# Attention in a hybrid decoder trunk: query norm factor moved into the exponential, head norm scales folded into keys and cosines, squares in one pass, two splits issued earlier

## The chip, the cores and the metric

The kernel runs on one core of one Trainium2 chip. The metric is the device time of one execution in microseconds (us). The engines are named as in the profile: PE (TensorE matmul; PEld its weight loads), DVE (VectorE), ACT (ScalarE), POOL (GpSimd) and SP (SyncE, which issues most DMAs).

## What is computed

Two layers over a sequence of 256 tokens of width 1024, in float32. Each layer has a SwiGLU feed-forward block, a token mixer and a second SwiGLU block. The mixer of layer 0 is a diagonal state-space model, that of layer 1 is attention with 8 heads of 128 columns. The change touches the attention alone:

```python
qkv = (h @ w_qkv).reshape(bsz, seq, 3, N_HEADS, HEAD_DIM)
q = rms_norm(qkv[:, :, 0], q_gain)      # over the 128 columns of each head
k = rms_norm(qkv[:, :, 1], k_gain)
q = partial_rope(q, cos, sin) * (HEAD_DIM ** -0.5)   # rotates columns 0..31
k = partial_rope(k, cos, sin)
...
s_own = jnp.einsum('bqhd,bkhd->bqhk', q_c, k_own)
s_own = jnp.where(causal, s_own, -jnp.inf)
...
p = jax.nn.softmax(jnp.concatenate(scores, axis=-1), axis=-1)
```

With 256 tokens there is one block of keys, so what is left of the block-sparse form is plain causal attention.

## The kernel before

Six stages follow one another: feed-forward, state-space mixer, feed-forward, feed-forward, attention, feed-forward. All large products keep float32 accuracy by splitting: a weight tile becomes a rounded high half `whi` and the rest `wlo`, the activations likewise `xa`, and a product is three matmuls (high by high, low by high, high by low).

Weights come by `Stream` (lines 37 to 117). A unit is a raw tile of 128x2048 that a DMA fills; it has two halves of 1024 columns. `split` (line 74) makes a half's `whi` on ACT (line 92, or line 86 where no norm scale is multiplied in) and its `wlo` on DVE (line 93 or 87). For the attention's first six weights each of these is two instructions of 128x512. In this text a split is such a pair on DVE with its pair on ACT. `pump` (line 103) does the next split ahead of its use if a buffer is free; nine pairs of buffers exist. Engines work through their own instruction lists in order, and the lists are written in the order in which the Python code runs: there is no scheduler behind it.

The attention stage is `moba` (line 1256). Its first part is twelve chunks, numbered 0 to 11 here: first half of the heads' keys, first half of the queries, second half of the keys, second half of the queries, two halves of the values, each for two blocks of 128 tokens (`QKV`, line 214). A chunk is eight steps `k` of three 512-column matmuls (`product`, line 429, matmuls at lines 439 to 441) and takes PE some 5.6 us without other work. After steps 1 and 5 `pump` splits one more half. Odd steps have hooks: four slots per chunk at which other work is put in, by the table `plan` (lines 1364 to 1378).

After a key or query chunk ACT evicts the product as `qs` (line 1278) and squares it head by head with a running sum (line 1282); POOL turns the four sums into norm factors `qrs` by six small instructions (line 1283 and `rsq`, lines 310 to 314). One chunk later, at the third slot, `rope` runs on DVE: four instructions scale each head by its factor and the norm scale (line 1293), six rotate the first 32 columns (lines 1299 to 1304). One further chunk later, at the third slot, `qk_tr` transposes the result on PE (line 1314; the last one a slot earlier) and ACT evicts it.

From chunk 6 on heads are added, each by `scores` (PE, then mask and maxima on DVE, lines 1324 to 1328), `expo` one slot later (two exponentials on ACT with sums), `normal` three slots after `scores` (reciprocal and two multiplications on DVE, lines 1343 to 1345), `p_tr` six slots after it (transposes of the probabilities on PE, line 1351, evicted by ACT) and `p_v` (product with the values). The second part of the stage, `mo`, is the output product.

```python
            for i in range(8):
                at(4 * (i + 1) + 2, rope, *prods[i])
                at(4 * (i + 2) + (2 if i < 7 else 1), qk_tr, *prods[i])
            for hd in range(8):
                g = 24 + 4 * hd if hd < 4 else 30 + 2 * hd
                for i, fn in ((0, scores), (1, expo), (3, normal), (6, p_tr)):
                    at(g + i, fn, hd)
```

Of the kernel before, what the change touches and what calls it, by code (L numbers as in the profile page):

```python
# [10 lines left out]
F32 = mybir.dt.float32  # L11
F32R = mybir.dt.float32r
AF = mybir.ActivationFunctionType
OP = mybir.AluOpType
AX = mybir.AxisListType
# [6 lines left out]
EPS = 1e-6  # L22
RAW = 3
HB = 9
NEG = -3.0e38
TWO_PI = 2.0 * math.pi
MAGIC = 12582912.0

# [92 lines left out]
def trunk_kernel(ctx: ExitStack, tc, x, ffn_norm, ffn_w_gate, ffn_w_up, ffn_w_down, mix_norm,  # L121
# [3 lines left out]
    nc = tc.nc  # L125
# [118 lines left out]
    cosT = cst[:, 256:288].rearrange("p (t f) -> p t f", t=2)  # L244
    sinT = cst[:, 288:320].rearrange("p (t f) -> p t f", t=2)
# [183 lines left out]
    def product(o, t, uA, uB, hooks, pumps=(1, 5)):  # L429

        for k in range(8):
            for f in hooks.get(k, ()):
                f()
            u = (uA, uB)[k // 4]
            wh, wl = st.get(u, (k % 4) // 2)
            c = slice((k % 2) * 512, (k % 2) * 512 + 512)
            ts = slice(t * 128, t * 128 + 128)
            xh, xl = X["h"][:, k, ts], X["l"][:, k, ts]
            mm(o, xh, woven(wh[:, c]), start=k == 0, stop=False)
            mm(o, xl, woven(wh[:, c]), start=False, stop=False)  # L440
# [815 lines left out]
    def moba(nxt):  # L1256
        V, P = nc.vector, nc.gpsimd
        SCL = 128 ** -0.5
        with tc.tile_pool(name="moba", bufs=1) as wp:
            gq = wp.tile([128, 2, 128], F32, name="gq")  # L1260
            for i, g in enumerate((moba_q_norm, moba_k_norm)):
                nc.sync.dma_start(gq[:, i, :], bass.AP(tensor=g.tensor, offset=g.offset,
                                                       ap=[[0, 128], [1, 128]]))
            vs = [wp.tile([128, D], F32, name=f"vs{t}") for t in range(2)]
            oa = wp.tile([128, 4224], F32R, name="oa")
            oh, ol = (oa[:, OO + 2048 * i:OO + 2048 * i + 2048].rearrange("p (k c) -> p k c", c=256)
                      for i in range(2))
            qkT, QS, QN, SC, PR, PT = {}, {}, {}, {}, {}, {}

            def chunk(kind, hh, t, hooks):  # L1270
                uA, uB = where[kind, hh, 0], where[kind, hh, 1]
                ps = psM()
                product(ps, t, uA, uB, hooks)
                if kind == "v":
                    nc.scalar.activation(halves(vs[t][:, hh * 512:(hh + 1) * 512]), unwoven(ps), AF.Identity, scale=Rr[t])
                    return
                qs = fp.tile([128, 512], F32, name="qs", tag="gr", bufs=2)
                nc.scalar.activation(halves(qs), unwoven(ps), AF.Identity, scale=Rr[t])
                ss = wp.tile([128, 4], F32, name="qss", bufs=2)
                sq = wp.tile([128, 128], F32, name="qsq", bufs=1)  # L1280
                for i in range(4):
                    nc.scalar.activation(sq, qs[:, i * 128:(i + 1) * 128], AF.Square, accum_out=ss[:, i:i + 1])
                P.tensor_scalar(ss, ss, 1.0 / 128, EPS, op0=OP.mult, op1=OP.add)
                rs = wp.tile([128, 4], F32, name="qrs", bufs=2)
                rsq(rs, ss, 4)
                QS[kind, hh, t] = (qs, rs)

            def rope(kind, hh, t):
                qs, rs = QS.pop((kind, hh, t))
                qn = wp.tile([128, 4, 128], F32, name="qn", bufs=2)  # L1290
                g = gq[:, 0 if kind == "q" else 1, :]
                for i in range(4):
                    V.scalar_tensor_tensor(qn[:, i, :], qs[:, i * 128:(i + 1) * 128], rs[:, i:i + 1], g,
                                           op0=OP.mult, op1=OP.mult)
                x1, x2 = qn[:, :, 0:16], qn[:, :, 16:32]
                cb = cosT[:, t, None, :].to_broadcast([128, 4, 16])
                sb = sinT[:, t, None, :].to_broadcast([128, 4, 16])
                m = [wp.tile([128, 4, 16], F32, name=f"rp{i}", bufs=1) for i in range(4)]
                V.tensor_tensor(m[0], x1, cb, op=OP.mult)
                V.tensor_tensor(m[1], x2, sb, op=OP.mult)  # L1300
                V.tensor_tensor(m[2], x2, cb, op=OP.mult)
                V.tensor_tensor(m[3], x1, sb, op=OP.mult)
                V.tensor_tensor(x1, m[0], m[1], op=OP.subtract)
                V.tensor_tensor(x2, m[2], m[3], op=OP.add)
                QN[kind, hh, t] = qn
# [11 lines left out]
            def scores(hd):  # L1317
                hh, i = divmod(hd, 4)
                q, k = qkT["q", hh], qkT["k", hh]
                ps = psA(i)  # L1320
                mm(ps[:, 0:128], q[:, i, 0:128], k[:, i, 0:128], start=True, stop=True)
                mm(ps[:, 128:384], q[:, i, 128:256], k[:, i, 0:256], start=True, stop=True)
                dv = ps.rearrange("p (a c) -> p a c", c=256)[:, :, 0:128]
                V.tensor_tensor(dv, dv, cmask[:, None, :].to_broadcast([128, 2, 128]), op=OP.add)
                mx = wp.tile([128, 2], F32, name="mx", bufs=3)
                V.reduce_max(mx[:, 0:1], ps[:, 0:128], axis=AX.X)
                V.reduce_max(mx[:, 1:2], ps[:, 128:384], axis=AX.X)
                V.tensor_scalar(mx, mx, -SCL, None, op0=OP.mult)
                SC[hd] = (ps, mx)

            def expo(hd):
                ps, mx = SC.pop(hd)
                pr = wp.tile([128, 384], F32, name="pr", bufs=4)
                sm = wp.tile([128, 2], F32, name="sm", bufs=4)
                nc.scalar.activation(pr[:, 0:128], ps[:, 0:128], AF.Exp, bias=mx[:, 0:1], scale=SCL,
                                     accum_out=sm[:, 0:1])
                nc.scalar.activation(pr[:, 128:384], ps[:, 128:384], AF.Exp, bias=mx[:, 1:2], scale=SCL,
                                     accum_out=sm[:, 1:2])
                PR[hd] = (pr, sm)

            def normal(hd):
                pr, sm = PR[hd]
                V.reciprocal(sm, sm)
                V.tensor_scalar(pr[:, 0:128], pr[:, 0:128], sm[:, 0:1], None, op0=OP.mult)
                V.tensor_scalar(pr[:, 128:384], pr[:, 128:384], sm[:, 1:2], None, op0=OP.mult)

            def p_tr(hd):
                pr, _ = PR.pop(hd)
# [30 lines left out]
            for i, (kind, hh, t) in enumerate(prods):  # L1379
                hooks = {2 * s + 1: plan.get((i, s), []) for s in range(4)}  # L1380
                if i == 0:
                    hooks.update(entry_hooks("moba"))
                chunk(kind, hh, t, hooks)
            acc = [None] * 4

            def mo(b, t, n, last=False):
# [165 lines left out]
```

## Time and profile before

| | |
|---|---|
| median of 3 runs | 921.55 us (921.38 to 924.65) |
| the profiled execution | 926.08 us |
| its span, first to last instruction | 924.3 us |
| mean granted TensorE clock | 0.997 |
| PE, PEld busy | 914.9 (99%), 817.9 (88%) |
| DVE, ACT, POOL busy | 719.0 (78%), 587.0 (64%), 222.7 (24%) |
| attention stage in the span | about 642 to 749 us |

Busy time is what the profiler saw an engine work; for PE the ends of matmuls are modelled and overlap, so that small gaps don't show there. A wait is idle time of an engine ahead of an instruction, put down to what released it. Times within the trace count from the span's start.

### The profile page before, as it was taken

To read this page: it belongs to the slowest core of one execution; us is meant where nothing else is said; L and a number is where in the kernel's file an instruction comes from. 1 tells how busy PE (TensorE), PEld (TensorE's weight loads), DVE (VectorE), ACT (ScalarE), POOL (GpSimd) and SP (SyncE) were. 2 spreads that over 40 slices of the span, in tenths; PEclk is the share of its full clock that TensorE was granted. 3 is DMA by queue.
4 is the path that set the end of the run, shared out by engine and by line. 5 is a ranking of instruction groups with operands and counts; after the bars stand their busy time and mean duration, and the time that the engine had idled before them with its cause. 6 is when DMAs were issued, how large, how long until landed. Compare 5 with 4: busy or idle time off the path is not lost.

```text
span 924.3 us, 15612 instructions
## 1 busy us (share of the span) xinstructions
PE 914.9 (99%) x5772; PEld 817.9 (88%) x5772; DVE 719.0 (78%) x1235; ACT 587.0 (64%) x1122; POOL 222.7 (24%) x389
## 2 busy tenths in 40 slices
PE   9999999999999999999999999999999999999998
PEld 7888878898999999999999999999888899999997
DVE  6899877868877888777678887776789668887773
ACT  7665756654376666666466666665898666676651
POOL 6992879924812000000020000001441020000000
PEclk9999999999999999999999999999999999999999
DMA  9999999988746766565637666563554647656531
GB/s 286 277 294 334 331 265 273 301 282 322 287 158 197 235 224 231 186 227 183 183 126 238 228 194 216 186 224 97 182 164 156 195 135 252 234 187 227 182 137 46
DMA packets 145388, 200.75 MB, mean 217 GB/s; under 512 B 20168, under 2 KB 117408, under 8 KB 145056
## 3 DMA queue, kind: packets, MB, share of 16 engines
q1 hardware_dynamic: 137744, 188.24, 62.6%
q0 software_dynamic: 6848, 10.72, 4.3%
q10 hardware_dynamic: 720, 0.80, 0.3%
q8 instruction: 45, 0.74, 0.3%
q14 instruction: 31, 0.25, 0.1%
HBM read 183.82 MB, written 15.76 MB: 216 GB/s over the span
## 4 chain that ended last, share of the span: by engine, by line
PE 89%; DMA 3%; POOL 2%; issue 2%; DVE 2%; ACT 1%; SPq 0%; ACTq 0%; DVEq 0%; POOLq 0%
PE pR L589 11%; PE pM L589 11%; PE pA L425 10%; PE pA L426 10%; PE pA L427 10%; PE pR L591 5%; PE pM L591 5%; PE pM L425 4%; PE pM L426 4%; PE pM L427 4%; PE pM L595 2%; PE pM L596 2%; PE pM L594 2%; DMA dA<-t 2%; PE pR L1118 1%
## 5 line engine op out<-in xcount | busy, mean ns | idle before, releaser
L93 DVE SCALAR_TENSOR_TENSOR wlo<-raw,gT,whi 128x512 fp32r<-128x512 f32 x328 | 228.0, 747 | 41.9 <-ACT whi L92 41.7
L87 DVE TENSOR_TENSOR wlo<-raw,whi 128x1024 fp32r<-128x1024 f32 (+1 forms) x155 | 188.0, 1233 | 41.4 <-ACT whi L86 37.0
L92 ACT ACTIVATE whi<-raw,gT 128x512 fp32r<-128x512 f32 x328 | 212.9, 710 | 3.5 <-PE pA L427 2.1
L86 ACT ACTIVATE whi<-raw 128x1024 fp32r<-128x1024 f32 (+1 forms) x155 | 158.5, 1045 | 38.3 <-DMA raw<-in_ffn_w_up_dram 25.5
L589 PE MATMUL pR<-xa,whi 128*128 128x512 f32 x456 | 174.2, 382 | 0.0
L589 PE MATMUL pM<-xa,whi 128*128 128x512 f32 x456 | 174.0, 382 | 0.0
L425 PE MATMUL pA<-whi,ah 128*128 128x512 f32 x352 | 134.9, 383 | 0.0
L426 PE MATMUL pA<-wlo,ah 128*128 128x512 f32 x352 | 133.7, 380 | 0.0
L427 PE MATMUL pA<-whi,al 128*128 128x512 f32 x352 | 133.6, 379 | 0.0
L591 PE MATMUL pR<-xa,wlo 128*128 128x256 f32 x456 | 124.3, 273 | 0.0
L591 PE MATMUL pM<-xa,wlo 128*128 128x256 f32 x456 | 124.3, 273 | 0.0
L355 POOL TENSOR_TENSOR ms<-ss 128x1 f32<-128x1 f32 x10 | 3.5, 348 | 435.4 <-ACT sq L352 435.4
L589 PEld LDWEIGHTS pR<-xa,whi 128*128 128x128 f32 x456 | 86.2, 189 | 12.2
L589 PEld LDWEIGHTS pM<-xa,whi 128*128 128x128 f32 x456 | 86.2, 189 | 11.9
L591 PEld LDWEIGHTS pM<-xa,wlo 128*128 128x128 f32 x456 | 87.4, 192 | 1.4
L591 PEld LDWEIGHTS pR<-xa,wlo 128*128 128x128 f32 x456 | 87.6, 192 | 0.0
L618 ACT ACTIVATE sg<-gr 128x256 f32<-128x256 f32 x66 | 27.5, 417 | 87.2 <-DVE gr L611 61.6
L425 PE MATMUL pM<-whi,xa 128*128 128x512 f32 (+1 forms) x208 | 79.9, 384 | 0.0
L426 PE MATMUL pM<-wlo,xa 128*128 128x512 f32 (+1 forms) x208 | 76.2, 366 | 0.1
L427 PE MATMUL pM<-whi,xa 128*128 128x512 f32 (+1 forms) x208 | 76.1, 366 | 0.0
L427 PEld LDWEIGHTS pA<-whi,al 128*128 128x128 f32 x352 | 66.7, 189 | 9.5
L425 PEld LDWEIGHTS pA<-whi,ah 128*128 128x128 f32 x352 | 66.8, 190 | 9.3
(290 smaller groups left out, 1745.1 us busy)
## 6 DMA issues: line engine op xcount, KB each, us to landing
raw<-in_ffn_w_down_dram SPq DMA_DIRECT2D x44, 1024.0 KB, 5.5
raw<-in_ffn_w_gate_dram SPq DMA_DIRECT2D x80, 512.0 KB, 4.0
raw<-in_ffn_w_up_dram SPq DMA_DIRECT2D x80, 512.0 KB, 5.1
raw<-in_moba_w_qkv_dram SPq DMA_DIRECT2D x12, 1024.0 KB, 5.2
TB<-dB SPq DMA_DIRECT2D x8, 768.0 KB, 7.0
dA<-blank SPq DMA_DIRECT2D x8, 512.0 KB, 10.2
dB<-tt POOLq DMA_DIRECT2D x16, 256.0 KB, 7.5
raw<-in_s_w_in_dram SPq DMA_DIRECT2D x4, 1024.0 KB, 9.7
```

The source lines that it names most:

```text
L86: nc.scalar.activation(hi[:, c], r[:, c], AF.Copy)
L87: nc.vector.tensor_tensor(lo[:, c], r[:, c], hi[:, c].bitcast(F32), op=OP.subtract)
L92: nc.scalar.activation(hi[:, c], r[:, c], AF.Identity, scale=g)
L93: nc.vector.scalar_tensor_tensor(lo[:, c], r[:, c], g, hi[:, c].bitcast(F32), op0=OP.mult, op1=OP.subtract)
L425: mm(o, xh, wh, start=start, stop=False)
L426: mm(o, xh, wl, start=False, stop=False)
L427: mm(o, xl, wh, start=False, stop=stop)
L589: mm(ps[i], a, XB[:, :, k, :].rearrange("p i (t c) -> p i c t", t=2), start=k == 0, stop=False, skip_group_check=True)
L591: mm(ps[i][:, 0:256], b, xh, start=False, stop=k == 7, skip_group_check=True)
L594: mm(o, a, xh, start=k == 0 and i == 0, stop=False, skip_group_check=True)
L595: mm(o, a, xl, start=False, stop=False, skip_group_check=True)
L618: nc.scalar.activation(sg, gr[:, 0, :], AF.Silu)
```

## The change

- The query's norm factor is no longer multiplied into the queries. It is a factor per token and head, so it goes into the scale of the exponential and into the maximum that is subtracted: POOL multiplies the factor by 128^-0.5 into `scl`, one instruction of 128x4 per query chunk.
- Both head norms' scales are folded: for columns 32 to 127 their product `gk` is multiplied into the keys alone; for the rotated columns each goes into its own copy of cosines and sines, `cs`. POOL makes both at the start of the stage, in ten instructions. So `rope` of a query chunk is the six rotations alone, and works in place on `qs`; `rope` of a key chunk still has the four scalings, with the product `gk`.
- The four squares with running sums become one ACTIVATE over 512 columns, and the sums a reduction on DVE.
- `normal` multiplies on ACT in place of DVE for heads 2 to 7; the reciprocal stays on DVE.
- Chunks 1 and 2 split one more half each, after step 3.
- The mask's value is -1e30 in place of -3e38, since it is now multiplied by a factor that differs from token to token.

```diff
+            gk = wp.tile([128, 128], F32, name="gk")
+            P.memset(gk[:, 0:32], 1.0)
+            P.tensor_tensor(gk[:, 32:128], gq[:, 0, 32:128], gq[:, 1, 32:128], op=OP.mult)
+            cs = wp.tile([128, 2, 4, 2, 16], F32, name="cs")
+            for i in range(2):
+                for m, (tr, c) in enumerate(((cosT, 0), (sinT, 16), (cosT, 16), (sinT, 0))):
+                    P.tensor_tensor(cs[:, i, m], tr, gq[:, i, None, c:c + 16].to_broadcast([128, 2, 16]), op=OP.mult)
...
-                sq = wp.tile([128, 128], F32, name="qsq", bufs=1)
-                for i in range(4):
-                    nc.scalar.activation(sq, qs[:, i * 128:(i + 1) * 128], AF.Square, accum_out=ss[:, i:i + 1])
+                sq = wp.tile([128, 512], F32, name="qsq", bufs=1)
+                nc.scalar.activation(sq, qs, AF.Square)
+                V.reduce_sum(ss, sq.rearrange("p (i c) -> p i c", c=128), axis=AX.X)
                 P.tensor_scalar(ss, ss, 1.0 / 128, EPS, op0=OP.mult, op1=OP.add)
                 rs = wp.tile([128, 4], F32, name="qrs", bufs=2)
                 rsq(rs, ss, 4)
+                if kind == "q":
+                    if t == 0:
+                        SQ[hh] = wp.tile([128, 4, 2], F32, name="scl", bufs=2)
+                    P.tensor_scalar(SQ[hh][:, :, t], rs, SCL, None, op0=OP.mult)
...
-                qn = wp.tile([128, 4, 128], F32, name="qn", bufs=2)
-                g = gq[:, 0 if kind == "q" else 1, :]
-                for i in range(4):
-                    V.scalar_tensor_tensor(qn[:, i, :], qs[:, i * 128:(i + 1) * 128], rs[:, i:i + 1], g,
-                                           op0=OP.mult, op1=OP.mult)
+                qn = qs.rearrange("p (i c) -> p i c", c=128)
+                if kind == "k":
+                    for i in range(4):
+                        V.scalar_tensor_tensor(qn[:, i, :], qn[:, i, :], rs[:, i:i + 1], gk, op0=OP.mult, op1=OP.mult)
...
-                V.tensor_scalar(mx, mx, -SCL, None, op0=OP.mult)
+                V.scalar_tensor_tensor(mx, mx, -1.0, SQ[hh][:, i, :], op0=OP.mult, op1=OP.mult)
...
-                nc.scalar.activation(pr[:, 0:128], ps[:, 0:128], AF.Exp, bias=mx[:, 0:1], scale=SCL,
+                nc.scalar.activation(pr[:, 0:128], ps[:, 0:128], AF.Exp, bias=mx[:, 0:1], scale=sc[:, 0:1],
                                      accum_out=sm[:, 0:1])
...
                 V.reciprocal(sm, sm)
-                V.tensor_scalar(pr[:, 0:128], pr[:, 0:128], sm[:, 0:1], None, op0=OP.mult)
-                V.tensor_scalar(pr[:, 128:384], pr[:, 128:384], sm[:, 1:2], None, op0=OP.mult)
+                for k, c in enumerate((slice(0, 128), slice(128, 384))):
+                    if hd < 2:
+                        V.tensor_scalar(pr[:, c], pr[:, c], sm[:, k:k + 1], None, op0=OP.mult)
+                    else:
+                        nc.scalar.activation(pr[:, c], pr[:, c], AF.Identity, scale=sm[:, k:k + 1])
...
-                chunk(kind, hh, t, hooks)
+                chunk(kind, hh, t, hooks, (1, 3, 5) if i in (1, 2) else (1, 5))
```

How this moves instructions on the engines is shown at three places.

The first is DVE in chunks 1 and 2, from the last split of chunk 0 on: `wlo` is a split, the `L1293` or `L1304` rows scale a key chunk, the rows after them (of six, the first is shown) rotate it. Before:

```order
L93 SCALAR_TENSOR_TENSOR wlo<-raw,gT,whi 128x512 x4
L1293 SCALAR_TENSOR_TENSOR qn<-qs,qrs,gq 128x128 x4
L1299 TENSOR_TENSOR rp_7453<-qn,cst 128x64
...
L93 SCALAR_TENSOR_TENSOR wlo<-raw,gT,whi 128x512 x4
L1293 SCALAR_TENSOR_TENSOR qn<-qs,qrs,gq 128x128 x4
```

With the change:

```order
L93 SCALAR_TENSOR_TENSOR wlo<-raw,gT,whi 128x512 x2
L1289 TENSOR_REDUCE qss<-qsq 128x4
L93 SCALAR_TENSOR_TENSOR wlo<-raw,gT,whi 128x512 x4
L1304 SCALAR_TENSOR_TENSOR qs<-qs,qrs,gk 128x128 x4
L1308 TENSOR_TENSOR rp_7468<-qs,cs 128x64
...
L93 SCALAR_TENSOR_TENSOR wlo<-raw,gT,whi 128x512 x2
L1289 TENSOR_REDUCE qss<-qsq 128x4
L93 SCALAR_TENSOR_TENSOR wlo<-raw,gT,whi 128x512 x4
L1304 SCALAR_TENSOR_TENSOR qs<-qs,qrs,gk 128x128 x4
```

Each chunk has a reduction between its splits, and two splits instead of one stand between that place and the scaling.

The second is DVE in chunk 6, where the second half of the keys is scaled while head 0's scores are masked and their maxima taken (`pA` is the scores' bank). Before:

```order
L93 SCALAR_TENSOR_TENSOR wlo<-raw,gT,whi 128x512 x2
L1324 TENSOR_TENSOR pA_7804<-pA_7804,cst 128x2x128
L1326 TENSOR_REDUCE mx<-pA_7804 128x1
L1327 TENSOR_REDUCE mx<-pA_7804 128x1
L1328 TENSOR_SCALAR mx<-mx 128x2
L93 SCALAR_TENSOR_TENSOR wlo<-raw,gT,whi 128x512 x2
L1293 SCALAR_TENSOR_TENSOR qn<-qs,qrs,gq 128x128 x4
```

With the change:

```order
L93 SCALAR_TENSOR_TENSOR wlo<-raw,gT,whi 128x512 x2
L1289 TENSOR_REDUCE qss<-qsq 128x4
L1333 TENSOR_TENSOR pA_7808<-pA_7808,cst 128x2x128
L1335 TENSOR_REDUCE mx<-pA_7808 128x1
L1336 TENSOR_REDUCE mx<-pA_7808 128x1
L1337 SCALAR_TENSOR_TENSOR mx<-mx,scl 128x2
L93 SCALAR_TENSOR_TENSOR wlo<-raw,gT,whi 128x512 x2
L1304 SCALAR_TENSOR_TENSOR qs<-qs,qrs,gk 128x128 x4
```

The reduction from which POOL makes the factors of the scaling stands directly ahead of the mask, behind a split.

The third is ACT in chunk 9, from the first exponential of head 3 to that of head 4. Before:

```order
L1335 ACTIVATE pr,sm<-pA_8076,mx 128x128
L1337 ACTIVATE pr,sm<-pA_8076,mx 128x256
L1353 ACTIVATE pT<-pR 128x384
L92 ACTIVATE whi<-raw,gT 128x512 x2
L1335 ACTIVATE pr,sm<-pA_8120,mx 128x128
```

With the change:

```order
L1345 ACTIVATE pr,sm<-pA_8068,mx,scl 128x128
L1347 ACTIVATE pr,sm<-pA_8068,mx,scl 128x256
L1366 ACTIVATE pT<-pR 128x384
L86 ACTIVATE whi<-raw 128x1024
L1358 ACTIVATE pr<-pr,sm 128x128
L1358 ACTIVATE pr<-pr,sm 128x256
L1345 ACTIVATE pr,sm<-pA_8112,mx,scl 128x128
```

Head 3's two normalizations stand ahead of head 4's exponential, and the split is already one of the next weight.

## Rows read from the trace of the kernel before

**Rows 1.** The page, busy time of each engine, share of the span, instructions
```profile
PE 914.9 (99%) x5772; PEld 817.9 (88%) x5772; DVE 719.0 (78%) x1235; ACT 587.0 (64%) x1122; POOL 222.7 (24%) x389
```

**Rows 2.** Waits of PE, 642 to 736 us: total, times, longest
```profile
PE pM L441 <- DVE wlo L93: 0.8, 3, 0.3
```

**Rows 3.** Timeline of PE: start, length, instruction, idle time ahead and releaser
```profile
655.70 0.38 PE L439 MATMUL pM<-whi,xa 128*128 128x512 f32 x1
655.91 0.38 PE L440 MATMUL pM<-whi,xa 128*128 128x512 f32 x1
656.54 0.48 PE L441 MATMUL pM<-wlo,xa 128*128 128x512 f32 x1 [0.24 <-DVE wlo L93]
...
695.38 0.38 PE L440 MATMUL pM<-whi,xa 128*128 128x512 f32 x1
696.08 0.48 PE L441 MATMUL pM<-wlo,xa 128*128 128x512 f32 x1 [0.33 <-DVE wlo L93]
```

**Rows 4.** Busy time by stretch: length, PE, PEld, DVE, ACT, POOL, clock, DMA, GB/s
```profile
642.20:700.00 57.80, 56.97 (x285) 48.57 (x284) 46.79 (x136) 52.73 (x139) 26.22 (x60) 1.00 0.50 159
700.00:735.00 35.00, 35.00 (x184) 30.80 (x183) 27.68 (x63) 24.23 (x54) 0.00 (x0) 1.00 0.48 163
```

**Rows 5.** Waits of DVE, 640 to 736 us
```profile
DVE qn L1293 <- POOL qrs L314: 5.7, 7, 0.9
```

**Rows 6.** Timeline of DVE, 651 to 688 us
```profile
651.26 1.42 DVE L93 SCALAR_TENSOR_TENSOR wlo<-raw,gT,whi 128x512 fp32r<-128x512 f32 x2 [2.81 <-ACT whi L92]
653.62 1.14 DVE L1293 SCALAR_TENSOR_TENSOR qn<-qs,qrs,gq 128x128 f32<-128x128 f32 x4 [0.94 <-POOL qrs L314]
...
655.74 2.73 DVE L93 SCALAR_TENSOR_TENSOR wlo<-raw,gT,whi 128x512 fp32r<-128x512 f32 x4
659.40 1.14 DVE L1293 SCALAR_TENSOR_TENSOR qn<-qs,qrs,gq 128x128 f32<-128x128 f32 x4 [0.93 <-POOL qrs L314]
...
678.87 1.41 DVE L93 SCALAR_TENSOR_TENSOR wlo<-raw,gT,whi 128x512 fp32r<-128x512 f32 x2
680.19 0.43 DVE L1324 TENSOR_TENSOR pA<-pA,cst 128x256 f32<-128x256 f32 x1
...
681.39 1.41 DVE L93 SCALAR_TENSOR_TENSOR wlo<-raw,gT,whi 128x512 fp32r<-128x512 f32 x2
683.16 1.14 DVE L1293 SCALAR_TENSOR_TENSOR qn<-qs,qrs,gq 128x128 f32<-128x128 f32 x4 [0.37 <-POOL qrs L314]
...
686.61 0.16 DVE L1343 RECIPROCAL sm<-sm 128x2 f32<-128x2 f32 x1
...
687.27 0.42 DVE L1324 TENSOR_TENSOR pA<-pA,cst 128x256 f32<-128x256 f32 x1
```

**Rows 7.** Timeline of ACT: first eviction, and last read of sums in chunks 0 and 5
```profile
648.19 0.69 ACT L1278 ACTIVATE qs<-pM,rr 128x512 f32<-128x512 f32 x1 [0.79 <-PE pM L441]
...
650.42 0.19 ACT L1282 ACTIVATION_READ_ACCUMULATOR qsq<-qs 128x1 f32 x1
...
678.92 0.19 ACT L1282 ACTIVATION_READ_ACCUMULATOR qsq<-qs 128x1 f32 x1
```

**Rows 8.** Groups of DVE by line: shape, count, busy, mean ns, idle before
```profile
L1327 DVE TENSOR_REDUCE mx<-pA 128x1 f32<-128x256 f32 x8 | 3.3, 414 | 0.0
```

**Rows 9.** Timeline of POOL: norm factors of chunk 0, power of chunk 1
```profile
650.70 0.20 POOL L1283 TENSOR_SCALAR qss<-qss 128x4 f32<-128x4 f32 x1 [3.57 <-ACT qsq L1282]
650.98 1.02 POOL L310 TENSOR_TENSOR qrs<-qss,nhalf 128x4 f32<-128x4 f32 x1
...
656.62 1.40 POOL L310 TENSOR_TENSOR qrs<-qss,nhalf 128x4 f32<-128x4 f32 x1
```

**Rows 10.** Group of ACT by line: shape, count, busy, mean ns, idle before
```profile
L1361 ACT ACTIVATE oa<-pR 128x256 fp32r<-128x256 f32 x8 | 3.1, 383 | 4.2 <-PE pR L1360 4.2
```

**Rows 11.** Timeline of PE: transposes of the second key chunk and of head 0
```profile
662.48 0.60 PE L1314 MATMUL pR<-cst,qn 128*128 128x128 f32 x4
...
687.50 0.49 PE L1351 MATMUL pR<-cst,pr 128*128 128x128 f32 x3
```

More of the change, by code (lines that the diff above doesn't have):

```diff
@@ L24 @@
 HB = 9
-NEG = -3.0e38
+NEG = -1.0e30
 TWO_PI = 2.0 * math.pi
@@ L1267, in moba, with chunk @@
                       for i in range(2))
-            qkT, QS, QN, SC, PR, PT = {}, {}, {}, {}, {}, {}
-            def chunk(kind, hh, t, hooks):
+            qkT, QS, QN, SC, PR, PT, SQ = {}, {}, {}, {}, {}, {}, {}
+            def chunk(kind, hh, t, hooks, pumps=(1, 5)):
                 uA, uB = where[kind, hh, 0], where[kind, hh, 1]
                 ps = psM()
-                product(ps, t, uA, uB, hooks)
+                product(ps, t, uA, uB, hooks, pumps)
                 if kind == "v":
@@ L1289, in rope @@
                 qs, rs = QS.pop((kind, hh, t))
-                qn = wp.tile([128, 4, 128], F32, name="qn", bufs=2)
-                g = gq[:, 0 if kind == "q" else 1, :]
-                for i in range(4):
-                    V.scalar_tensor_tensor(qn[:, i, :], qs[:, i * 128:(i + 1) * 128], rs[:, i:i + 1], g,
-                                           op0=OP.mult, op1=OP.mult)
+                qn = qs.rearrange("p (i c) -> p i c", c=128)
+                if kind == "k":
+                    for i in range(4):
+                        V.scalar_tensor_tensor(qn[:, i, :], qn[:, i, :], rs[:, i:i + 1], gk, op0=OP.mult, op1=OP.mult)
                 x1, x2 = qn[:, :, 0:16], qn[:, :, 16:32]
-                cb = cosT[:, t, None, :].to_broadcast([128, 4, 16])
-                sb = sinT[:, t, None, :].to_broadcast([128, 4, 16])
+                c1, s2, c2, s1 = (cs[:, "qk".index(kind), k, t, None, :].to_broadcast([128, 4, 16]) for k in range(4))
                 m = [wp.tile([128, 4, 16], F32, name=f"rp{i}", bufs=1) for i in range(4)]
[L1299 to L1302, printed above, removed]
+                V.tensor_tensor(m[0], x1, c1, op=OP.mult)
+                V.tensor_tensor(m[1], x2, s2, op=OP.mult)
+                V.tensor_tensor(m[2], x2, c2, op=OP.mult)
+                V.tensor_tensor(m[3], x1, s1, op=OP.mult)
                 V.tensor_tensor(x1, m[0], m[1], op=OP.subtract)
@@ L1332, in expo @@
                 ps, mx = SC.pop(hd)
+                sc = SQ[hd // 4][:, hd % 4, :]
                 pr = wp.tile([128, 384], F32, name="pr", bufs=4)
                 sm = wp.tile([128, 2], F32, name="sm", bufs=4)
-                nc.scalar.activation(pr[:, 0:128], ps[:, 0:128], AF.Exp, bias=mx[:, 0:1], scale=SCL,
+                nc.scalar.activation(pr[:, 0:128], ps[:, 0:128], AF.Exp, bias=mx[:, 0:1], scale=sc[:, 0:1],
                                      accum_out=sm[:, 0:1])
-                nc.scalar.activation(pr[:, 128:384], ps[:, 128:384], AF.Exp, bias=mx[:, 1:2], scale=SCL,
+                nc.scalar.activation(pr[:, 128:384], ps[:, 128:384], AF.Exp, bias=mx[:, 1:2], scale=sc[:, 1:2],
                                      accum_out=sm[:, 1:2])
```

## The prediction

> **What bounds the kernel now.** I read the page first: TensorE (PE) is busy in 99% of the span [rows 1]. Its busy time is modelled, so it hides small gaps, and the next view is who waits for whom on PE in the attention stage, 642 to 736 us. It lists one wait alone, 0.8 us in three places, on VectorE's (DVE) low half of a weight split [rows 2]. The third view, PE in order of time, shows what that view rounds away: two 512-column matmuls start 0.21 to 0.22 us apart, and in four places the product by the low half starts late. At 656.54 the step is 0.63 instead of 0.215, a loss of 0.41; at 668.10 and 682.19, read in the same way, 0.22 and 0.35; at 696.08 it is 0.70, a loss of 0.49 [rows 3]. Together 1.48 us, 0.16% of the time. All that the change touches lies in this stage, the clock stands at its upper level, 2.4 GHz, there (granted share 1.00, [rows 4]), and PE's own instructions keep their number and order. So the most that can be won is 1.48 us, and whatever is won or lost must show as a wait of PE.
>
> Why is DVE late in those places? It is busy 46.8 of 57.8 us, ScalarE (ACT) 52.7 [rows 4], and DVE's own longest wait is for GpSimd (POOL): 5.7 us in seven places, ahead of the head norm's scaling [rows 5]. The chain is: ACT evicts a product and squares it, POOL makes the norm factor, DVE scales and rotates, PE transposes one chunk later. The rows give DVE's prices, from start to start: a split 1.33 (678.87 to 680.19, rounded up), a scaling with its rotation 2.12 (653.62 to 655.74), of which the four scalings are 1.14 and the rotation 0.98, mask and maxima of one head 1.20 (680.19 to 681.39), reciprocal and two normalizations 0.66 (686.61 to 687.27) [rows 6].
>
> **The change, part by part.**
>
> Squares: four squares with running sums become one ACTIVATE over 512 columns. In the first chunk the four took from the eviction's end at 648.88 (648.19 + 0.69) to 650.61 (650.42 + 0.19), 1.73 us. The one costs at most the 0.69 of the eviction of the same size [rows 7], at least a quarter of the four, 0.43; I take 0.68 with its gap, so it ends at 649.56, 1.05 earlier. By itself none of that is on the path.
>
> The sum moves to DVE: eight new reductions of 128x512 into four numbers. The trace has none of this size; the nearest takes 0.41 for 256 elements [rows 8]. Ends: 0.41, as if length cost nothing, and 0.83, twice the row; it can't gain anything by itself. I take 0.62, halfway. What matters more is the place. The sum was ready as soon as ACT was; now POOL must wait until DVE comes to the reduction, behind the splits in its queue.
>
> Query chunks: four scalings go, 1.14 us of DVE each time, four times, and with them the rotation's wait for POOL. Key chunks keep both. The query's factor goes into the exponential's scale; the two extra operand reads and the four small POOL instructions have a whole stage of cover, so nothing.
>
> POOL's ten preparing instructions (the product of the two norm scales, the scaled cosines) stand ahead of the first norm factor. POOL was idle for 3.57 us before its first instruction of this kind, at 650.70 [rows 9], and ten of 0.2, as that one took, are 2.0. Held by splits for 0.4 each, as the power instruction was (1.40 - 1.02), they would be 6. I count nothing; the other end, 2.4 us, would delay the first key chunk and is kept for the range.
>
> Two more splits, one in chunk 1, one in chunk 2: 2.66 us of DVE work comes earlier, and from there each split is one chunk ahead of its use. This removes all four waits of [rows 3]: -1.48. But the rotation of the same chunk now stands behind two splits of its chunk instead of one, and its deadline has not moved.
>
> Normalization of heads 2 to 7 on ACT: DVE is relieved of some 0.5 per head (0.66 less the reciprocal's 0.16), ACT takes at most 2 x 0.38 by the copy of 256 columns [rows 10], covered by its idle time, 35.0 - 24.2 = 10.8 us after 700 [rows 4].
>
> **What is late next.** Two deadlines of PE: the transposes of the second key chunk at 662.48, and those of head 0's probabilities at 687.50 [rows 11]; without the earlier losses of 0.41 and of 0.99 they stand at 662.07 and 686.51. DVE's list from the first reduction to the end of head 0's normalization is now 14 splits (18.62), 4 scalings with rotation (8.48), 2 rotations (1.96), 6 reductions (3.72), one head's maxima (1.20) and normalization (0.66): 34.64 us. To it come waits for POOL at the four key chunks. From the squares' end to the scaling POOL's chain took 653.62 - 650.61 = 3.0 with one split beside it and 683.16 - 679.11 = 4.05 with two splits and a head's maxima [rows 6, 7]; I take 3.4, between them and nearer the first, since the third of the four new chains again has one split beside it. DVE fills 2.66, 2.66, 1.33 and 2.53 of the four chains with splits and maxima, so it waits 0.74 + 0.74 + 2.07 + 0.87 = 4.42.
>
> To test the method, the list before: from 651.26, 12 splits, 6 scalings with rotation, maxima and normalization are 30.54, the waits 0.94 at 653.62, 0.93 in the four chunks from 659.40 on and 0.37 at 683.16, in sum 5.03; that ends at 686.83, and the row says 687.27 [rows 6]. It is 0.44 short, which I add.
>
> The list after: 649.56 + 34.64 + 4.42 + 0.44 = 689.06, against 686.51: new waits of PE of 2.55 us. The first part of them is at the key transposes: 649.56 + 13.6 = 663.2 against 662.07, some 1.1 us; the rest, 1.4, ahead of head 0's transposes. After that DVE has 0.5 less per head and the queries don't wait, so I count no further loss. Sum: -1.48 + 2.55 = **+1.1 us**.
>
> The bounds: with 0.41 per reduction and 3.0 per chain the list ends 2.9 earlier, no new wait is left, -1.5. With 4.05 per chain it ends 2.6 later, +3.7; with 0.83 per reduction as well, 1.3 more, +4.9.
>
> The profiled execution took 926.08 (span 924.3), 4.5 more than the median of the runs, 921.55; by the sum it becomes 927.2. The runs differ by up to 3.3 us among themselves, and I put the same difference on the median: 921.55 + 1.1 = 922.6.
>
> **A rule weighed.** POOL's power instruction took 1.02 us at 650.98, and 1.40 at 656.62, when it began beside a split [rows 9]. The Trainium skill, in SBUF — State Buffer, section Who interferes with whom, says that a VectorE instruction with two inputs in SBUF and a GpSimd instruction that reads SBUF exclude each other for the whole instruction, whichever began first. The trace agrees. By that rule a chain that starts together with two or more queued splits would be held at nearly every step; the sum would be +3.7 by it and +1.1 by the rows' usual chain. This is the second rival.
>
> **The rivals.**
> - *No new wait* (chance 0.25): reductions near 0.41 and chains of 3.0. For it: ACT ends its squares 1.05 earlier, and DVE is relieved of 1.14 in each query chunk. Against it: the reductions stand behind splits. 921.55 - 1.48 = 920.1.
> - *POOL is held by the splits* (0.17), slower than before: in chunks 1 and 2 two splits stand right behind the reduction, so POOL's six instructions of each key chunk run beside them. The price is a chain of 4.05 in place of 3.4; it decides as soon as the chain is over about 3.0, from which on each tenth costs four. 921.55 + 3.7 = 925.2. For it the row of 4.05, against it the chains that had a split beside them and took less.
> - *ACT is held by the reciprocals* (0.08): the normalization now stands in ACT's queue ahead of a later head's exponential and of a split, and waits for DVE's reciprocal. If each of six heads held ACT for a split's time, 6 x (0.77 + 1.33) = 12.6 us would meet 10.8 of idle time: 1.8 more than the forecast, 924.4. Against it: the transposes come three slots of a quarter chunk after the normalization, and 16 slots lie between the two rows of [rows 11]: three are 3 x 25.0 / 16 = 4.7 us.
> - *The change doesn't do what it says* (0.05): the earlier splits wait for data or a free buffer and nothing moves: 921.55.
>
> **How the numbers follow.** My forecast, new waits of about 2.55 us for 1.48 removed, has 0.45. A measurement of this kernel can tell about 0.5%, 4.6 us, from no change: under 917.0 or over 926.2. No case reaches the first (0.02 for what I don't see); the second is reached by the corner of the second rival with 0.83 per reduction, 0.06. The remaining 0.92 is within. The range goes from a little under the first rival, 919.8, to the second, 925.3.
>
> **What would show it.** Right: no wait of PE for a low half in this stage; a wait of about 1 us at the transposes of the second key chunk, near 662 us, released by DVE's rotation; another of 1 to 2 us at 687 to 689; reductions of some 0.65 us on DVE; rotations of the queries without a wait for POOL, and waits of some 2 us at the third key chunk. Wrong: transposes that don't wait (first rival), POOL's chain at 4 us everywhere (second), exponentials that wait on ACT behind a normalization (third), or a time below 919 or above 927, for which I have no mechanism.

## The result, and the profile after the change

The changed kernel takes 931.16 us (median of 6 runs, 929.54 to 933.16), the one before 921.79 in runs of the same sitting: 1.0088 times as long, 95% interval 1.0064 to 1.0111, or 8.1 us more (5.9 to 10.2); the two medians by themselves lie 9.4 apart, and all differences below go by the ratio. The forecast was 922.6, and its range ended at 925.3.

The profiled execution took 931.57 us, its span is 929.9. That is only 5.5 more than the profiled execution of before, because that one had a loss of its own in an earlier stage. From one matmul to the same later one PE takes 6.69 us there (131.36 to 138.05) and 2.81 in the changed kernel's trace (132.31 to 135.12), 3.9 less; this part of the kernel isn't changed. The waits of PE in before's trace from 130 to 140 us, and the busy time by stretch (columns as in [rows 4]):

```profile
PE pR L527 <- ACT kt L956: 2.0, 1, 2.0
```
```profile
133.00:138.00 5.00, 4.29 (x13) 3.48 (x14) 4.72 (x5) 4.73 (x9) 3.96 (x6) 0.66 0.86 250
```

So the accounts below go by stretches of the attention stage, not by the two spans.

The page of after, engines as in [rows 1]: the totals hardly move, and PE is still at 98%.

```profile
PE 915.5 (98%) x5772; PEld 819.1 (88%) x5772; DVE 717.7 (77%) x1215; ACT 585.6 (63%) x1078; POOL 222.3 (24%) x403
```

The waits of PE, 642 to 740 us, against [rows 2]:

```profile
PE pR L1372 <- ACT pT L1366: 1.9, 1, 1.9
PE pR L1323 <- DVE qs L1313: 1.7, 1, 1.7
PE pA L1331 <- ACT qT L1324: 1.6, 1, 1.6
PE pR L1364 <- ACT whi L92: 1.2, 1, 1.2
PE pR L1364 <- ACT pT L1366: 0.9, 1, 0.9
PE pR L1372 <- DVE oa L1375: 0.2, 1, 0.2
```

The wait for a low half is gone, as forecast. Six others stand in its place. The timeline of PE gives their places (`...` stands for rows left out):

```profile
658.58 0.38 PE L441 MATMUL pM<-wlo,xa 128*128 128x512 f32 x1
660.66 0.66 PE L1323 MATMUL pR<-cst,qs 128*128 128x128 f32 x4 [1.70 <-DVE qs L1313]
...
686.27 0.61 PE L1364 MATMUL pR<-cst,pr 128*128 128x128 f32 x3 [1.16 <-ACT whi L92]
...
702.03 0.70 PE L1331 MATMUL pA<-kT,qT 128*128 128x256 f32 x2 [1.61 <-ACT qT L1324]
...
718.04 0.55 PE L1364 MATMUL pR<-cst,pr 128*128 128x128 f32 x3 [0.93 <-ACT pT L1366]
...
718.77 0.70 PE L1372 MATMUL pR<-pT,vs 128*128 128x256 f32 x2 [0.18 <-DVE oa L1375]
...
722.84 1.03 PE L1372 MATMUL pR<-pT,vs 128*128 128x256 f32 x2 [1.85 <-ACT pT L1366]
...
724.95 0.63 PE L441 MATMUL pM<-wlo,xa 128*128 128x512 f32 x1
725.38 0.63 PE L425 MATMUL pA<-whi,oa 128*128 128x512 f32 x1
...
726.23 0.51 PE L427 MATMUL pA<-whi,oa 128*128 128x512 f32 x1
```

Read as in the forecast (each step from start to start, less the step without a wait), they cost 1.86, 1.40, 1.86, 1.09, 0.43 and 2.02 us: 3.26 at the first two places, which the forecast named, and **5.40 after 700 us, which it did not**. The label of the second, ACT's high half of a weight, is not its cause: head 0's transposes don't read that weight. They read `pr`, which DVE normalizes from 685.84 on, and with the old squares (below) the same wait is gone. After the last one the matmuls start 0.43 apart instead of 0.216, and the stretch shows why:

```profile
642.20:700.00 57.80, 54.95 (x277) 47.63 (x276) 50.13 (x136) 44.54 (x81) 29.84 (x67) 1.00 0.54 182
700.00:735.00 35.00, 30.42 (x146) 25.51 (x145) 18.30 (x37) 24.87 (x57) 0.00 (x0) 0.95 0.33 109
722.80:726.50 3.70, 3.66 (x10) 3.00 (x11) 1.73 (x3) 2.27 (x6) 0.00 (x0) 0.54 0.60 195
```

The granted clock is 0.54 there, nearly the lower level of 1.2 GHz. From 722.84 to 726.23 is 3.39 us; the same instructions at the upper level took 1.84 (below, with the old squares), so this is 1.55 more. Sum: the new waits, the clock, less the 1.48 of low-half waits that went: 8.66 + 1.55 - 1.48 = 8.7 us, which is the measured difference within its interval.

Why ACT is late after 700 is seen in its waits, 695 to 730 us, of which this is the longest:

```profile
ACT pr L1358 <- DVE sm L1353: 8.1, 6, 1.4
```

Six times, once per moved head, ACT stands ahead of a normalization until DVE has the reciprocal. One round on ACT, and then the same round on DVE:

```profile
712.76 1.07 ACT L86 ACTIVATE whi<-raw 128x1024 fp32r<-128x1024 f32 x1
715.25 0.80 ACT L1358 ACTIVATE pr<-pr,sm 128x128 f32<-128x128 f32 x2 [1.43 <-DVE sm L1353]
715.96 0.44 ACT L1345 ACTIVATE pr<-pA,mx,scl 128x128 f32<-128x128 f32 x1
...
717.87 0.39 ACT L1374 ACTIVATE oa<-pR 128x256 fp32r<-128x256 f32 x1
718.14 1.07 ACT L86 ACTIVATE whi<-raw 128x1024 fp32r<-128x1024 f32 x1
```
```profile
713.86 1.23 DVE L87 TENSOR_TENSOR wlo<-raw,whi 128x1024 fp32r<-128x1024 f32 x1 [0.52 <-ACT whi L86]
715.00 0.16 DVE L1353 RECIPROCAL sm<-sm 128x2 f32<-128x2 f32 x1
...
718.29 0.42 DVE L1375 TENSOR_TENSOR oa<-pR,oa 128x256 fp32r<-128x256 f32 x1 [1.96 <-ACT oa L1374]
```

ACT makes a high half (1.07); DVE can make the low half only then (1.23); the reciprocal is queued behind it (0.16); ACT's next instruction is the normalization that needs the reciprocal. So ACT idles 1.43 for a 0.16 us instruction that could have run long before: the exponential it belongs to had ended ahead of the high half. Then ACT does the exponentials and evictions, and DVE waits 1.96 for one of them. The two engines take turns. This round, the longest, takes 5.4 us from one high half to the next (712.76 to 718.14); the four from 703.22 to 722.95 take 19.7.

### The profile page after: what moved, and what is told of

Same layout as the page of the kernel before. It is cut to its first block, busy times and chain, and to the rows that moved or that the text cites. A ratio compares the mean times of both kernels' runs of the same rounds, so it can differ in the third digit from the quotient of the medians.

```text
span 929.9 us, 15566 instructions
## 1 busy us (share of the span) xinstructions
PE 915.5 (98%) x5772; PEld 819.1 (88%) x5772; DVE 717.7 (77%) x1215; ACT 585.6 (63%) x1078; POOL 222.3 (24%) x403
## 4 chain that ended last, share of the span: by engine, by line
PE 85%; DVE 5%; ACT 4%; DMA 3%; POOL 2%; issue 1%; ACTq 0%; SPq 0%; DVEq 0%
PE pR L589 11%; PE pM L589 11%; PE pA L425 9%; PE pA L426 9%; PE pA L427 9%; PE pM L591 5%; PE pR L591 5%; PE pM L425 4%; PE pM L426 3%; PE pM L427 3%; PE pM L595 2%; PE pM L596 2%; PE pM L594 2%; DMA raw<-in_ffn_w_up_dram 2%; PE pR L1118 1%
```

## Experiments

Theory A: the loss after 700 us is ACT's wait for the reciprocal, a matter of place in two queues. Rivals: B, the late start at 660 and 686 us carries on into the later waits; C, ACT has too much work; D, the early splits do it. Each ratio is to the kernel before, run on the same chip as the experiment.

**Normalizations back on DVE.**

```diff
-                for k, c in enumerate((slice(0, 128), slice(128, 384))):
-                    if hd < 2:
-                        V.tensor_scalar(pr[:, c], pr[:, c], sm[:, k:k + 1], None, op0=OP.mult)
-                    else:
-                        nc.scalar.activation(pr[:, c], pr[:, c], AF.Identity, scale=sm[:, k:k + 1])
+                V.tensor_scalar(pr[:, 0:128], pr[:, 0:128], sm[:, 0:1], None, op0=OP.mult)
+                V.tensor_scalar(pr[:, 128:384], pr[:, 128:384], sm[:, 1:2], None, op0=OP.mult)
```

> The changed kernel with all normalizations back on DVE (heads 2 to 7 too), the rest of the change kept. Theory A, ACT is held by the reciprocals: in the changed kernel's trace PE loses 1.86 us at 702, 1.09 + 0.43 at 718, 2.02 at 722.8, and some 2.3 more at a granted clock of 0.54 behind that, 7.7 us in sum; all of it goes: 931.2 - 7.7 = 923.5 (922.5 to 924.5), and no wait of PE is left after 700; the waits at 660 (1.86) and 686 (1.40) stay. Theory B, the reductions on DVE and POOL's chain behind them make the stage late at 660 and 686, and the later waits only follow from that: over 929. Theory C, ACT simply has too much work: the 0.80 us per head that it sheds is 4.8 us, all of which comes back at best: 926 to 927.

Measured: 925.33 us, ratio 1.0022 (1.0010 to 1.0034), 2.0 us above the kernel before instead of 8.1. All its waits of PE from 642 to 740 us:

```profile
PE pR L1323 <- DVE qs L1313: 1.7, 1, 1.7
PE pR L1361 <- ACT whi L92: 1.2, 1, 1.2
```

The two early waits are there as before (1.86 and 1.40), and nothing follows from them. B falls: they are not the cause of the later ones.

**The moved normalization alone**, in the kernel before: its two multiplications in `normal` replaced by the loop of the change.

> The kernel before with one part of the change alone: the normalization of heads 2 to 7 on ACT. Theory A: this alone loses most of it, with waits of ACT for DVE's reciprocal and of PE for ACT's evictions after 700 us; 4 to 8 us slower than before: 926 to 930. Theory B: no late start here, so at most 1 us: 921.5 to 923. Theory D, the two early splits shift every split by one chunk and so put one ahead of each reciprocal: without them nothing happens either, 921.5 to 923; B and D are told apart by the next run.

Measured: 928.80, ratio 1.0057 (1.0042 to 1.0072), 5.3 us slower. ACT's longest wait, 695 to 730 us:

```profile
ACT pr L1348 <- DVE sm L1343: 9.1, 6, 2.6
```

The one part brings most of the loss by itself, 5.3 of 8.1, and does so without early splits: D falls as its cause.

**The reciprocal one slot earlier**: the changed kernel, ACT's work unchanged.

```diff
+            def recip(hd):
+                if hd >= 2:
+                    sm = PR[hd][1]
+                    V.reciprocal(sm, sm)
+
             def normal(hd):
                 pr, sm = PR[hd]
-                V.reciprocal(sm, sm)
+                if hd < 2:
+                    V.reciprocal(sm, sm)
...
-                for i, fn in ((0, scores), (1, expo), (3, normal), (6, p_tr)):
+                for i, fn in ((0, scores), (1, expo), (2, recip), (3, normal), (6, p_tr)):
```

> The changed kernel, with the reciprocals of heads 2 to 7 one slot earlier in DVE's order, that is ahead of the split whose high half stands ahead of the normalization on ACT. ACT does exactly the work of the changed kernel; only the place of a 0.16 us instruction on DVE moves. Theory A, the wait and not the work is what costs: the six waits of ACT (1.0 + 5 x 1.4 us) go nearly wholly, and the time comes down to that of the kernel with all normalizations on DVE, 2 to 3.5 us above the kernel before. Theory C, ACT has too much work: no change, 8 to 9.5 us above the kernel before. Rival to both: DVE now waits for the exponentials' sums instead, and the splits behind it are late; then low-half waits appear on PE, 4 to 7 us above.

Measured: 924.77, ratio 1.0027 (1.0016 to 1.0039), 2.5 us above the kernel before. The round of ACT and of DVE with the same instructions as the one above:

```profile
708.02 1.05 ACT L86 ACTIVATE whi<-raw 128x1024 fp32r<-128x1024 f32 x1
708.96 0.79 ACT L1364 ACTIVATE pr<-pr,sm 128x128 f32<-128x128 f32 x2
...
711.97 0.38 ACT L1380 ACTIVATE oa<-pR 128x256 fp32r<-128x256 f32 x1 [0.27 <-PE pR L1379]
712.25 1.05 ACT L86 ACTIVATE whi<-raw 128x1024 fp32r<-128x1024 f32 x1
```
```profile
706.69 0.17 DVE L1354 RECIPROCAL sm<-sm 128x2 f32<-128x2 f32 x1 [0.44 <-ACT pr L1347]
...
709.10 1.22 DVE L87 TENSOR_TENSOR wlo<-raw,whi 128x1024 fp32r<-128x1024 f32 x1 [0.40 <-ACT whi L86]
```

The normalization starts as the high half ends, and the low half runs beside it. The round takes 4.2 us instead of 5.4, and the four from 700.71 to 715.82 take 15.1 instead of 19.7. Of the four waits of PE after 700 one is left, that for the eviction of the queries' transposes, 0.85 instead of 1.86. With the normalizations on DVE it isn't there, so this much is left of C; it is gone too in the last kernel of this section, which has the same normalizations without the reductions and the early splits. DVE does wait for the exponentials' sums, 0.44 here, but no wait of PE for a low half follows. The same work takes 5.6 us less, and the ratio, 1.0027, lies within the interval of that with the work on DVE (1.0010 to 1.0034): A is shown, and C falls but for the 0.85.

**No early splits**, the rest of the change kept (`chunk(kind, hh, t, hooks)` in the loop over the chunks).

> The changed kernel without the two early splits. Theory A: the loss after 700 stays, since each head still has a split between the high half on ACT and the reciprocal on DVE; the waits at 660 and 686 (3.26 us) shrink by the one split of 1.33 that is ahead of them, and the low-half waits of 1.48 come back in part: 928 to 931. Theory D, the early splits cause the loss: 921 to 924.

Measured: 932.06, ratio 1.0088 (1.0064 to 1.0112). The wait at the key transposes shrinks to 0.66 and the one at head 0's goes, but low-half waits of 0.44, 1.27 and 0.99 come back: even the early waits are only exchanged. The time is above the 928 to 931 expected for A, and the runs spread from 928.04, at a mean granted clock of 1.0, to 936.24 at 0.993: part of it is likely the clock, but the one trace is of the fastest run.

**The four old squares**, the rest kept.

```diff
-                sq = wp.tile([128, 512], F32, name="qsq", bufs=1)
-                nc.scalar.activation(sq, qs, AF.Square)
-                V.reduce_sum(ss, sq.rearrange("p (i c) -> p i c", c=128), axis=AX.X)
+                sq = wp.tile([128, 128], F32, name="qsq", bufs=1)
+                for i in range(4):
+                    nc.scalar.activation(sq, qs[:, i * 128:(i + 1) * 128], AF.Square, accum_out=ss[:, i:i + 1])
```

> The changed kernel with the four squares with running sums on ACT again and no reduction on DVE. POOL's chain no longer stands behind DVE's queue: the waits at 660 and 686 (1.86 + 1.40) go wholly or nearly. Theory A: nothing else changes, 931.2 - 3.3 = 928 (927 to 929.5), with the waits after 700 still there. Theory B: with the early waits the later ones go too, 921 to 924.

Measured: 928.85, ratio 1.0067 (1.0048 to 1.0086). The early waits fall from 3.26 to 1.15 (0.28 and 0.87 at the key transposes), the later ones stay: 1.53, 1.09, 0.43, 2.02. Its PE after the last of them, which gave the 1.84 us above (718.83 to 720.67), and the stretch:

```profile
718.83 0.70 PE L1372 MATMUL pR<-pT,vs 128*128 128x256 f32 x2 [1.86 <-ACT pT L1366]
...
720.67 0.38 PE L427 MATMUL pA<-whi,oa 128*128 128x512 f32 x1
```
```profile
718.80:722.50 3.70, 3.67 (x18) 3.27 (x19) 1.72 (x3) 2.27 (x6) 0.00 (x0) 1.00 0.66 202
```

**What the other parts are worth.** Four kernels with all normalizations on DVE: folded factors and early splits, with the old squares; the same with later transposes, `at(4 * (i + 2) + (3 if i < 2 else 2 if i < 7 else 1), qk_tr, *prods[i])`; folded factors alone; folded factors with the new squares.

> The changed kernel with the four old squares and all normalizations on DVE: what is left of the change are the folded factors and the two early splits. If the parts add up, the waits after 700 and at 686 are gone, those of the key transposes of 0.28 and 0.87 us (as with the old squares alone) stay, and the four low-half waits (1.48) stay gone: 0.3 us below the kernel before (-1.0 to +0.5). If the reductions on DVE are not what makes the key transposes late, but the early splits, these two waits stand here unchanged; if theory B holds more than thought, they are gone.

Measured: 921.43, ratio 0.9987 (0.9970 to 1.0004). The parts add up in their waits: 0.28 and 0.87, no other. Without the early splits (folded factors alone, below) neither is there, so they are the early splits' own.

> As the run before in this call, with the transposes of the first two key chunks one slot later, where nothing waits for them. If the two waits of 0.28 and 0.87 us are only a deadline set too early, they go, and with the four low-half waits gone too no wait of PE is left in the stage: 1.5 us below the kernel before (-2.0 to -0.8). If the lateness only travels down DVE's queue, a wait for a low half appears behind it: 0 to 0.5 below.

Measured: 922.30, ratio 0.9999 (0.9985 to 1.0013). Neither expectation held. The two waits are gone, no low-half wait appears, but head 0's transposes now wait:

```profile
PE pR L1361 <- DVE pr L1354: 0.9, 1, 0.9
```

By steps it is 1.10, about the 1.15 that went. That fits a DVE that is late by its whole list, which PE meets at whichever deadline comes first.

> The folded factors alone: old squares, all normalizations on DVE, no early splits. DVE loses 1.14 us per query chunk and a wait for POOL there. If the early splits are what removes the four low-half waits, those of chunks 2 and 4 stand as before (0.41 and 0.22), and the ones behind the query chunks shrink: 0.3 to 1.0 below the kernel before. If DVE's relief by the queries alone does it, all four are gone: 1.5 below.

Measured: 921.77, ratio 0.9982 (0.9966 to 0.9998). One wait of PE is left in the stage:

```profile
653.35 0.48 PE L441 MATMUL pM<-wlo,xa 128*128 128x512 f32 x1 [0.24 <-DVE wlo L93]
```

The expectations were at least two of the four low-half waits left, or none. Folding alone removes three, with DVE relieved in the query chunks; no early split is needed for them.

> Folded factors and the new squares (one pass on ACT, the sums on DVE), all normalizations on DVE, no early splits; it differs from the kernel with the folded factors alone by the squares only. If the reductions on DVE are a cost of their own, the low-half waits of 0.44, 1.27 and 0.99 and the key transposes' wait of 0.66, seen in the changed kernel without early splits, stand here too: 3.4 against 1.5 us in the kernel before, 1.9 above it (+1.0 to +2.5). If those waits came from the normalizations on ACT, only some 0.4 is left: 1 below.

Measured: 925.41, ratio 1.0019 (1.0006 to 1.0032). The waits are those of the changed kernel without early splits: 0.43, 1.27, 0.99 for low halves, 0.68 at the key transposes. Against the folded factors alone the new squares cost some 3.4 us (1.0019 - 0.9982). DVE's waits for POOL in the four key chunks, 640 to 730 us, with the folded factors alone and then here:

```profile
DVE qs L1304 <- POOL qrs L314: 3.2, 4, 0.9
```
```profile
DVE qs L1304 <- POOL qrs L314: 7.4, 4, 2.6
```

So DVE has eight reductions of 0.62 us more to do, and waits 4.2 us longer for the chain that starts at them. The runs don't tell these two apart.

**Early splits alone**, in the kernel before; one early split after step 7 of chunk 1, with folded factors; and the folded factors with the normalizations on ACT and the early reciprocals.

> The kernel before with the two early splits alone. If they do what the forecast took from them, the four low-half waits (1.48) go, and the key transposes wait 0.3 and 0.9 us, as in the kernel with folded factors and early splits; the queries' scalings, 1.14 each, are still there, so the list to head 0's transposes is 2 to 4 us longer than there and may be late too: 0.3 below to 2 above the kernel before. Theory D, they cause the loss by themselves: 4 us or more above.

Measured: 923.85, ratio 1.0003 (0.9987 to 1.0019). The four low-half waits go; 0.37 and 0.81 at the key transposes and 0.71 at a later head's come in their place.

> The folded factors alone, with one early split instead of two, put after step 7 of chunk 1, behind the first key chunk's rotation. With the factors folded one low-half wait of 0.41 is left; if a split that stands behind the rotation removes it without delaying a transpose, no wait of PE is left in the stage: 1.5 below the kernel before (-2.2 to -0.8). If the second key chunk's transposes become late instead, as with two splits, 0.5 to 1.0 below.

Measured: 922.25, ratio 0.9984 (0.9970 to 0.9999). Neither held in its waits: the low-half wait of 0.41 stays, and the key transposes wait 0.28 besides.

> Folded factors with the old squares and no early splits, and the normalizations of heads 2 to 7 on ACT as in the change, with their reciprocals one slot earlier on DVE. Theory A: with the wait taken out, the moved multiplications are covered by ACT's idle time, as the forecast had it, and bring nothing either, since no wait of PE after 700 was left to remove: within 1 us of the kernel with the folded factors alone, 2.5 to 0.5 us below the kernel before. Theory C, the work itself costs: some of the waits of PE for ACT's evictions after 700 are back, 1 to 4 us above the kernel before.

Measured: 921.99, ratio 0.9989 (0.9978 to 1.0000). The only wait of PE of the stage is the 0.41 of the folded factors alone, though ACT has 29.10 us of work after 700, where the kernel before had 24.23 [rows 4]:

```profile
700.00:735.00 35.00, 35.00 (x185) 30.89 (x184) 23.78 (x49) 29.10 (x66) 0.00 (x0) 1.00 0.48 160
```

All kernels, by the waits of PE in the stage of the profiled execution (sum of the steps' excess), that sum less before's 1.48, and the measured ratio times 921.8:

| kernel | waits, us | against before | measured against before |
|---|---|---|---|
| changed | 8.66 | +7.2, +1.55 clock | +8.1 |
| without early splits | 7.64 | +6.2 | +8.1 |
| old squares | 6.22 | +4.7 | +6.2 |
| normalization on ACT alone | 6.31 | +4.8 | +5.3 |
| changed, early reciprocal | 4.11 | +2.6 | +2.5 |
| changed, normalization on DVE | 3.26 | +1.8 | +2.0 |
| folded, new squares | 3.38 | +1.9 | +1.8 |
| early splits alone | 1.89 | +0.4 | +0.3 |
| folded, early splits | 1.15 | -0.3 | -1.2 |
| the same, later transposes | 1.10 | -0.4 | -0.1 |
| folded, one early split | 0.69 | -0.8 | -1.5 |
| folded, ACT, early reciprocal | 0.41 | -1.1 | -1.0 |
| folded alone | 0.41 | -1.1 | -1.7 |

The view that the forecast rested on, PE's late starts, accounts for these times within 1 us, and each interval is some 1 to 2 us to either side. The two that stand further off, without early splits and with the old squares, have a wait of 2 us and a lower mean clock in several of their runs. A sum that needs no choice of steps agrees within some 0.6 us: from the first matmul of the stage (642.2 in the kernel before) to the same one near its end (734.9) PE takes 92.65 us before, 101.35 changed, 94.08 with the normalizations on DVE, 94.75 with the early reciprocal, 91.42 with the folded factors alone.

The folded factors alone beat both kernels: the changed one by about 1% (0.9982 against 1.0088), the one before by 0.2%, with an interval that ends just short of no difference.

## Why the prediction was wrong, point by point

- **The failed step** is the term for the moved normalization, put at nothing: that ACT's added work is "covered by its idle time, 35.0 - 24.2 = 10.8 us", and with it "I count no further loss" after head 0. The added work, 0.80 us per head, was indeed covered (29.10 of 35 us and no wait after 700, last experiment). What was not counted is the wait that came with it: a normalization on ACT needs a reciprocal from DVE, and that stood behind the low half of the split whose high half was directly ahead on ACT. Idle time as a sum says nothing on this; the order of both queues does, and it was in the piece of ACT's order that was printed: a split, then the normalization. That cost 5.40 us of waits, and behind the last of them the profiled execution lost 1.55 us more at the lower clock.
- **The third rival had this mechanism and a price far too small.** It set 12.6 us of holding against 10.8 of idle time, and took the difference, 1.8. The measured hold was smaller, 8.1, and cost 5.40 of waits. Each hold delays what is queued behind it (exponentials, evictions of transposes and of products, the next high half, and through it DVE), and PE waits for each of these at its own time. The argument against this rival looked at the transposes of the normalized head alone, 4.7 us later; the waits after 700 are for ACT's evictions and for DVE's step behind one. The hold's length at one head against the slack at that head was the comparison to make. With the early reciprocal ACT idles for 0, 0.70, 0.27 and 0.16 us in the four rounds from 700.71 to 715.82, and a hold there is 1.43. Of the 10.8 us of idle time in the kernel before, only 2.9 lay in the same four rounds (703.94 to 718.28, ACT busy for 11.47 of 14.34 us).
- **The four low-half waits: right.** They are gone in every kernel with the two early splits and, three of them, with the folded factors alone.
- **The second key chunk's transposes: right in place, 1.86 instead of 1.1.** DVE took 14.12 us from the first reduction to the end of the rotation (646.40 to 660.52), forecast 13.6:

```profile
646.40 0.69 DVE L1289 TENSOR_REDUCE qss<-qsq 128x4 f32<-128x512 f32 x1 [0.98 <-ACT qsq L1288]
647.02 2.74 DVE L93 SCALAR_TENSOR_TENSOR wlo<-raw,gT,whi 128x512 fp32r<-128x512 f32 x4
650.69 1.14 DVE L1304 SCALAR_TENSOR_TENSOR qs<-qs,qrs,gk 128x128 f32<-128x128 f32 x4 [0.94 <-POOL qrs L314]
...
658.40 1.14 DVE L1304 SCALAR_TENSOR_TENSOR qs<-qs,qrs,gk 128x128 f32<-128x128 f32 x4 [0.94 <-POOL qrs L314]
...
660.52 1.41 DVE L93 SCALAR_TENSOR_TENSOR wlo<-raw,gT,whi 128x512 fp32r<-128x512 f32 x2
...
686.30 0.68 DVE L1289 TENSOR_REDUCE qss<-qsq 128x4 f32<-128x512 f32 x1
```

  The waits for POOL are 0.94, 0.94, 2.32 and 0.65 in the four key chunks, forecast 0.74, 0.74, 2.07 and 0.87. A reduction takes 0.62 from start to start (646.40 to 647.02), as taken.
- **Head 0's transposes: right, 1.40 for 1.4.** DVE's whole list, to the end of head 0's normalization, took 39.90 us (646.40 to 686.30), forecast 39.50 (34.64 + 4.42 + 0.44). With the normalizations on DVE the rest of the change costs 2.0 us (0.9 to 3.1), forecast 1.1: that half of the working stands.
- **POOL's ten preparing instructions: right.** The last eight (2.17 from 644.83) end at 647.00, and the first norm factor starts at 647.18, when its sum is there.
- **The first rival**, no new wait, fell: a reduction takes 0.62 and not 0.41, and the chains take more than 3.0. Even without the reductions the two early splits leave 1.15 of waits.
- **The second rival**, POOL held at every step, fell too, by less. POOL's first step takes 0.62 beside a split and 0.19 without one, but the chain as a whole took 3.67, 3.66, 3.72 and 3.25 in the four key chunks (the first from 647.02 to 650.69), between the 3.4 taken and the 4.05 of the rival, three of them about halfway. The rule of the Trainium skill cited there (SBUF — State Buffer, Who interferes with whom) is borne out on both sides, unequally. A split pair mostly took 1.41, with POOL idle (660.52) and beside POOL's chain (662.44). Beside POOL's product of the two norm scales one took 1.54 (643.88): its second instruction has 0.88 us instead of the usual 0.74 to 0.76. Every kernel here with the folded factors has this one long split, the kernel before and the two built on it without folding have none.

```profile
643.88 1.54 DVE L93 SCALAR_TENSOR_TENSOR wlo<-raw,gT,whi 128x512 fp32r<-128x512 f32 x2
```
```profile
643.98 0.90 POOL L1266 TENSOR_TENSOR gk<-gq 128x96 f32<-128x96 f32 x1
...
654.91 0.62 POOL L1290 TENSOR_SCALAR qss<-qss 128x4 f32<-128x4 f32 x1 [4.25 <-DVE qss L1289]
...
679.12 0.19 POOL L1290 TENSOR_SCALAR qss<-qss 128x4 f32<-128x4 f32 x1 [4.25 <-DVE qss L1289]
```

## What to carry to other kernels

Before moving work to an engine with idle time, write out both queues around it: what the moved instruction needs from another engine, and what stands ahead of that over there. If that work itself waits for something queued ahead of the moved instruction, the two engines take turns, and the hold comes once per use, whatever the sum of idle time says. The cure here was to issue the small producer earlier: reciprocals of 0.16 us, one slot ahead, gave back 5.6 of the 8.1 us. And a sum that is moved into a busy queue costs its place there as well as its length: eight reductions of 0.62 us went with 4.2 us more of waiting for the chains that start at them, and cost 3.4 us in time.

## What the runs showed beyond that

- A wait of PE may be paid twice. After waits of 0.93, 0.18 and 1.85 us within 6 us, the changed kernel's profiled execution ran at a granted clock of 0.54 from 722.8 to 726.5, 1.55 us more. The kernel before shows the same behind its wait of 1.98 us: 0.50, the lower level of 1.2 GHz, from 135 to 137 us. But with the old squares the same three waits (0.93, 0.18, 1.86) were followed by 1.00. So not every execution pays it, and that may be what widens the spread of kernels with long waits (928.04 to 936.24 without early splits); no trace of the slower runs shows it.
- An exponential whose scale is an operand takes longer than one with a constant: 0.45 instead of 0.37 us for 128 columns, 0.55 instead of 0.47 for 256. From the groups of ACT by line and shape of after, and then of before:

```profile
L1345 ACT ACTIVATE pr<-pA,mx,scl 128x128 f32<-128x128 f32 x8 | 3.6, 446 | 2.2 <-DVE mx L1337 2.2
```
```profile
L1335 ACT ACTIVATE pr<-pA,mx 128x128 f32<-128x128 f32 x8 | 2.9, 366 | 3.4 <-DVE mx L1328 3.4
```
